# Token factors of two RMSNorms: from narrow sums, a 3-column root and row products to one wide product with a matrix of ones

## The chip, the cores and the metric

The kernel runs on one core of a Trainium2 chip. TensorE does the matrix products (weights are loaded into it beside the products), VectorE and ScalarE the operations on rows, GpSimd a few additions and some of the DMA issues, SyncE issues most DMAs. The metric is the device time of one execution in microseconds; lower is better. The times of before are three runs, 1497.79, 1493.73 and 1493.14 us, with the median 1493.73 us.

## The reference, cut to what matters

One step of a decoder trunk with one layer: a hybrid mixer, an attention into memory tokens, an MLP with squared ReLU, and a final norm. 1024 prompt tokens and 8 decode tokens go through the same weights, 1032 tokens in all. The model width is 1024, the hidden width 4096, and everything is f32. The change touches the two norms at the end:

```python
def rmsnorm(x, g):
    xf = x.astype(jnp.float32)
    y = xf * lax.rsqrt(jnp.mean(xf * xf, axis=-1, keepdims=True) + EPS)
    return (y * g.astype(jnp.float32)).astype(x.dtype)

def sq_relu_mlp(h, w_up, w_down):
    return jnp.square(jax.nn.relu(h @ w_up)) @ w_down

    ...
    xp = xp + sq_relu_mlp(rmsnorm(xp, norm_mlp[l]), w_up[l], w_down[l])
    ...
y_prompt = rmsnorm(xp, norm_final)
y_sample = rmsnorm(xd, norm_final)
```

Each token has one factor, 1 / sqrt(mean of its squares + EPS), which multiplies all 1024 of its values.

## The kernel before

**Layout.** Activations lie with the model width on the 128 partitions (8 tiles of 128) and the tokens along the columns. The 1032 tokens are four quarters of 258 columns (`QCOLS[0..3]`). A quarter pair is called a chunk `c`: chunk 0 has the quarters 0 and 1, chunk 1 the quarters 2 and 3. A token's factor must therefore come out as a row of numbers that stands on all 128 partitions.

**Products.** Every f32 operand is split into a high part and a low part (a rounding copy on ScalarE, written `UH`, `T_h` or the first half of `wu`, and a subtraction on VectorE, `UL`, `T_l`, the second half of `wu`), and each product is three passes: high by high, high by low, low by high. The MLP's two matrix products are done with a seven-product scheme over 2 x 2 blocks. `up_block(b, W, chunks)` runs the seven products of block b in the order 1, 6, 2, 7, 5, 4, 3. They share three PSUM banks: 1 and 2 add into X, 6, 7 and 4 into Z, 5 and 3 into Y. A product is 12 instructions of 258 columns (4 tiles of the width, 3 passes).

**What stands between the products (L2143).** After product 1, ScalarE copies X to `p` (L2194); product 2 adds into the same bank, so it must wait for that copy. After product 6, VectorE makes `u` from Z and `p` (L2197); product 7 adds into Z and must wait for `u`. Later results are added to `p` or `u` (L2206), multiplied by the factor row `ssum` under a ReLU (L2168), squared by ScalarE (`hq`), and combined into `ht` (L2176 to 2179), which goes to memory for the second matrix product.

**How the factor is made.** While the mixer's and the memory attention's result `pr_m` leaves PSUM, ScalarE squares each tile and GpSimd adds the squares, so that the quarter's 128 x 258 tile `ssum` holds one partial sum for each partition. `factor_columns` (L1979) multiplies that tile, as weights in three pieces of 86 tokens, by one column of ones (L1984): three narrow products that leave the token sums as a 86 x 3 block. ScalarE takes the root with the mean's scale and EPS as bias (L1988), VectorE the reciprocal (L1989), each on 3 columns. Later `factor_rows` turns that block into a row on all partitions with three products against an identity (through the helper, L75). `norm_rows` copies this row over `ssum` (L2004 in the function; on ScalarE). For the final norm VectorE multiplies from the PSUM bank directly.

**Where.** In the MLP, `norm_factor(0)` and `(1)` stand before the last of the `pr_m` products (n == 30), and their rows behind product 2 of block 0, chunk 0. Block 0 takes chunk 0 first, then come `norm_factor(2)` and `(3)`, the operands of chunk 1 (`first_half`, `second_half`), and block 0 for chunk 1 with its rows behind its product 2; from block 1 on both chunks run together. In the second matrix product (`dn`, L2309) the last of the output tiles `c` come at the program's end. `finish_columns` and `finish_rows` stand at four steps there (tables `COLUMNS_AT`, `ROWS_AT`, L2264), for each chunk and half of it: columns at steps 0, 3, 10 and 15, rows at 2, 5, 12 and 15. For the halves 1 the last tile's squares `sqt` are not added to `ssumf` but are multiplied by the ones in a second group of products into the same bank.

**What sets the order.** On TensorE the order is that of the text: `pin` keeps it so, and `pinned` and the helper `mm` hold the narrow and the row products in it. On ScalarE and VectorE a scheduler orders the instructions by its own estimate of when their operands are ready; so an edit can move instructions that it does not touch. Each engine then works off its own list in order and waits at its head.

Of the kernel before, what the change touches and what calls it, by code (L numbers as in the profile page):

```python
# [10 lines left out]
F32 = mybir.dt.float32  # L11
F32R = mybir.dt.float32r
I32 = mybir.dt.int32
AF = mybir.ActivationFunctionType
# [5 lines left out]
P = 128  # L20
D = 1024
# [5 lines left out]
QC = HALF // 2  # L27

QCOLS = [slice(h * HALF + c * QC, h * HALF + c * QC + QC) for c in range(2) for h in range(2)]
# [19 lines left out]
def decoder_step(ctx: ExitStack, tc: tile.TileContext, i: dict, o: dict):  # L49
    nc = tc.nc  # L50
# [10 lines left out]
    def pinned(ins):  # L61

        if pin[0]:
            tc.keep_in_program_order(ins)
# [9 lines left out]
    def mm(out, l, r, start, stop):  # L74
        pinned(nc.tensor.matmul(out, l, r, start=start, stop=stop))  # L75
# [20 lines left out]
    ones = G.tile([P, 1], F32, tag="ones", name="ones")  # L96
    nc.vector.memset(ones, 1.0)
    half = G.tile([P, 1], F32, tag="half", name="half")
# [182 lines left out]
    with pool("s") as A:  # L281
# [51 lines left out]
        ident = const("ident", [P, P])  # L333
# [12 lines left out]
        for t in range(9):  # L346
            n = P if t < 8 else 8
# [38 lines left out]
    with pool("a") as A:  # L386
# [29 lines left out]
        for t in range(9):  # L416
            q = A.tile([P, 512], F32, tag=f"qk{t}", name=f"qk_{t}")
# [1556 lines left out]
        nc.vector.tensor_sub(l, src, h.bitcast(F32))  # L1974


    QP = QC // 3

    def factor_columns(bank, sums, last, x):  # L1979
        col = bank[:QP, 300:303]  # L1980

        terms = [(y, j) for y in (sums, last) if y is not None for j in range(3)]
        for n, (y, j) in enumerate(terms):
            pinned(nc.tensor.matmul(  # L1984
                col[:, j : j + 1], y[:, j * QP : j * QP + QP], ones[:, :1], start=n == 0, stop=n >= len(terms) - 3,
                skip_group_check=True))
        fc = KC.tile([QP, 3], F32, tag=f"fc{x % 2}", name=f"fc_{x}", bufs=2)
        nc.scalar.activation(fc, col, AF.Sqrt, scale=1.0 / D, bias=epsc[:QP])  # L1988
        nc.vector.reciprocal(fc, fc)  # L1989
        return fc  # L1990

    def factor_rows(bank, fc):
        for j in range(3):
            mm(bank[:, j * QP : j * QP + QP], fc[:, j : j + 1].to_broadcast([QP, P]), ident[:QP, :QP], True, True)
        return bank[:, :QC]

    FACTORS = {}

    def norm_factor(x):
        fp = PD.tile([P, 512], F32, tag=("mk", "dt")[x % 2], name=f"rm_{x}", bufs=1)  # L2000
        FACTORS[x] = fp, factor_columns(fp, ssum[:, QCOLS[x]], None, x)

    def norm_rows(x):
        nc.scalar.copy(ssum[:, QCOLS[x]], factor_rows(*FACTORS[x]))  # L2004

    def first_half(c):

# [141 lines left out]
    def up_block(b, W, chunks):  # L2149
# [32 lines left out]
        for q in (1, 6, 2, 7, 5, 4, 3):  # L2182
            for c in chunks:
                if q in (1, 6, 5):
                    kind, d = {1: ("X", X), 6: ("Z", Z), 5: ("Y", Y)}[q]
                    d[c] = bank(kind, c)
                ps = (X if q in (1, 2) else Z if q in (6, 7, 4) else Y)[c]
                product(W, q, c, ps, q in (1, 6, 5))
                if b == 0 and q == 2:
                    norm_rows(2 * c)  # L2190
                    norm_rows(2 * c + 1)
                if q == 1:
                    p1[c] = small("p1", c)
                    nc.scalar.copy(p1[c], ps)  # L2194
                elif q == 6:
                    u2[c] = small("u2", c)
                    nc.vector.tensor_add(u2[c], ps, p1[c])  # L2197
                elif q == 2:
                    hidden(11, ps, c)
                elif q == 7:  # L2200
                    u3[c] = small("u3", c)
                    nc.vector.tensor_add(u3[c], ps, p1[c])
                else:
                    quad, x = {5: (22, u3), 4: (21, p1), 3: (12, u2)}[q]
                    r = small("r", f"{quad}_{c}", 4)
                    nc.vector.tensor_add(r, ps, x[c])  # L2206
                    hidden(quad, r, c)
# [33 lines left out]
    with pool("acc", side="right") as AC, pool("rd", side="right") as RD, pool("w") as A, pool("w_ps", space=PSUM) as PS:  # L2241
# [81 lines left out]
            nc.scalar.activation(sq, x, AF.Square)  # L2323
            (nc.vector if quad in (22, 12) else nc.gpsimd).tensor_add(ssf[:, cs], ssf[:, cs], sq)

        ends = {}

        def finish_columns(c, half):
            fp = PS.tile([P, 512], F32, tag=f"acc{turns[0] % 8}", name=f"fin_{c}_{half}", bufs=1)
            turns[0] += 1  # L2330
            ends[c, half] = fp, factor_columns(fp, ssf[:, QCOLS[2 * c + half]], tails[c] if half else None, 4 + 2 * c + half)
            for ft in range(8):
                y = C[((11, 21), (12, 22))[half][ft // 4]][:, ft % 4, c * QC : c * QC + QC]
                nc.scalar.activation(y, y, AF.Copy, scale=g_fin[:, ft : ft + 1])

        def finish_rows(c, half):
            cs = QCOLS[2 * c + half]
            rf = factor_rows(*ends[c, half])
            n = 2 if (c, half) == (1, 1) else 4
            for ft in range(0, 8, n):  # L2340
                y = C[((11, 21), (12, 22))[half][ft // 4]][:, ft % 4 : ft % 4 + n, c * QC : c * QC + QC]
                nc.vector.tensor_mul(y, y, rf.unsqueeze(1).to_broadcast([P, n, QC]))
                (nc.scalar if n == 2 and ft % 4 else nc.sync).dma_start(
                    o["yT"][ft * P : (ft + n) * P, cs].rearrange("(f p) c -> p f c", p=P), y)
# [282 lines left out]
```

## Time and profile before

| | |
|---|---|
| median of 3 runs | 1493.73 us (1493.14 to 1497.79) |
| span of the profiled execution | 1492.5 us |
| TensorE products | 1474.0 us busy, 99% of the span |
| TensorE weight loads (beside the products) | 1402.5 us, 94% |
| VectorE | 1102.5 us, 74% |
| ScalarE | 678.4 us, 45% |
| GpSimd | 325.4 us, 22% |

The profile gives the span of the profiled execution as its own time, from its first to its last instruction; the runs' times are taken on the device around the whole execution. Lines of the profile are read so: a start in us, a length in us, the engine, the line of the kernel, what is written `<-` what is read, the shape, and in brackets how long the engine stood idle before and what ended that. PE is TensorE, PEld its weight load, DVE VectorE, ACT ScalarE. In the chain of waits each row is a stretch on the chain that ended last: start, length, engine and what it did. In the groups by line, the two numbers behind the first bar are the group's busy us and the mean ns of one.

Of the places named above, `pr_m` ends and block 0 begins near 829 us, chunk 1 of block 0 runs from near 842 us, and the steps of the final norm stand between 1457 us and the end.

### The profile page before, as it was taken

Reading aid. Unit: us, or ns where it says so; the run is one execution under the profiler, and the core shown is the slowest. Engines: PE = TensorE matmul, PEld = TensorE weight load, DVE = VectorE, ACT = ScalarE, POOL = GpSimd, SP = SyncE. Lnnn points to the kernel's source line nnn. Section 1 sums busy time; section 2 is a strip of 40 time slices with the busy share of each in tenths; the row PEclk is TensorE's granted clock in tenths of the full one; section 3 lists DMA queues with packets and bytes.
Section 4 is the critical chain, followed back from the end, with each engine's and each line's share of the span. In section 5 each row is a group of like instructions: output and inputs, shape, how many; then the busy total and the mean of one; then the engine's idle time right before and its main releaser. Section 6 shows DMA issues by size and latency. Waiting matters only on the chain.

```text
span 1492.5 us, 27826 instructions
## 1 busy us (share of the span) xinstructions
PE 1474.0 (99%) x10893; PEld 1402.5 (94%) x10893; DVE 1102.5 (74%) x2279; ACT 678.4 (45%) x1326; POOL 325.4 (22%) x346
## 2 busy tenths in 40 slices
PE   9999999998999999999999999999999999999997
PEld 7899779998769999989999999999999999999997
DVE  7656636987877734567786978888888889787875
ACT  7534435665652432147535634334344444343454
POOL 0035323114414321104132000000001311020380
PEclk9999999999999999999999999999999999999999
DMA  8155737214857157483592443344436674536273
GB/s 292 61 186 168 201 71 181 80 34 123 232 181 279 49 191 193 132 238 103 165 321 72 128 149 137 141 156 157 142 141 210 237 265 142 172 99 191 81 129 114
DMA packets 125229, 236.67 MB, mean 159 GB/s; under 512 B 13744, under 2 KB 76517, under 8 KB 124970
## 3 DMA queue, kind: packets, MB, share of 16 engines
q1 hardware_dynamic: 89056, 170.50, 36.5%
q0 software_dynamic: 24912, 44.80, 10.9%
q10 hardware_dynamic: 11130, 19.60, 3.5%
q8 instruction: 85, 1.39, 0.4%
q14 instruction: 46, 0.38, 0.1%
HBM read 170.24 MB, written 57.52 MB: 153 GB/s over the span
## 4 chain that ended last, share of the span: by engine, by line
PE 90%; DVE 5%; ACT 2%; issue 1%; DMA 1%; ACTq 0%; POOL 0%; DVEq 0%; SPq 0%
PE dn L2309 21%; PE Z L2143 9%; PE qkp L75 7%; PE pr_o L75 6%; PE mq L75 6%; PE pr_m L75 6%; PE X L2143 6%; PE Y L2143 6%; PE grp L75 3%; PE sp L75 2%; PE av L75 2%; PE mv L75 2%; PE mk L75 1%; PE mpv L75 1%; PE vap_z L522 1%
## 5 line engine op out<-in xcount | busy, mean ns | idle before, releaser
L2309 PE MATMUL dn<-UH,wd 128*128 128x258 f32 x1792 | 324.6, 283 | 0.0
L2309 PEld LDWEIGHTS dn<-UH,wd 128*128 128x128 f32 x1792 | 277.5, 189 | 0.7 <-ACT c L2410 0.2
L2309 PE MATMUL dn<-UL,wd 128*128 128x258 f32 x896 | 252.8, 282 | 0.0
L2309 PEld LDWEIGHTS dn<-UL,wd 128*128 128x128 f32 x896 | 169.0, 189 | 0.0
L2413 DVE TENSOR_TENSOR c<-c,dn 128x258 f32<-128x258 f32 x216 | 88.9, 418 | 38.5 <-PE dn L2309 36.1
L2169 ACT ACTIVATE hq<-r 128x258 f32<-128x258 f32 x128 | 53.7, 421 | 118.3 <-DVE r L2168 118.3
L2143 PE MATMUL Z<-T_h,wu 128*128 128x258 f32 x512 | 98.2, 284 | 0.0
L2143 PE MATMUL X<-UH,wu 128*128 128x258 f32 x512 | 97.4, 282 | 0.0
L2287 ACT CAST wd<-raw_d 128x512 fp32r<-128x512 f32 x96 | 58.8, 620 | 79.0 <-PE dn L2309 74.6
L1953 ACT CAST wu<-raw_up 128x512 fp32r<-128x512 f32 x96 | 59.1, 617 | 59.9 <-PE Z L2143 50.0
L2280 ACT CAST UH<-raw_h 128x1032 fp32r<-128x1032 f32 x56 | 58.7, 1056 | 53.5 <-PE dn L2309 27.7
L2143 PEld LDWEIGHTS X<-UH,wu 128*128 128x128 f32 x512 | 81.3, 188 | 0.2 <-ACT p L2194 0.2
L2143 PEld LDWEIGHTS Z<-T_h,wu 128*128 128x128 f32 x512 | 81.3, 189 | 0.0
L2180 POOL DMA_DIRECT2D HT<-ht x32 | 17.2, 538 | 292.3 <-DVE ht L2179 291.8
L2281 DVE TENSOR_TENSOR UL<-raw_h,UH 128x1032 fp32r<-128x1032 f32 x56 | 73.6, 1315 | 8.6 <-ACT UH L2280 8.6
L2288 DVE TENSOR_TENSOR wd<-raw_d,wd 128x512 fp32r<-128x512 f32 x96 | 72.2, 759 | 10.0 <-ACT wd L2287 9.9
L2143 PE MATMUL Z<-T_l,wu 128*128 128x258 f32 x256 | 72.3, 282 | 0.0
L2143 PE MATMUL X<-UL,wu 128*128 128x258 f32 x256 | 72.3, 282 | 0.0
L128 ACT CAST wh_u<-raw_u 128x1024 fp32r<-128x1024 f32 x43 | 44.6, 1047 | 54.3 <-PE mq L75 31.1
L1954 DVE TENSOR_TENSOR wu<-raw_up,wu 128x512 fp32r<-128x512 f32 x96 | 64.7, 687 | 3.5 <-ACT wu L1953 3.5
L2301 POOL TENSOR_TENSOR raw_d<-raw_d,raw_d 128x512 f32<-128x512 f32 x16 | 22.1, 1383 | 193.8 <-DVE raw_d L2297 172.9
L129 DVE TENSOR_TENSOR wl_u<-raw_u,wh_u 128x1024 fp32r<-128x1024 f32 x39 | 49.4, 1273 | 18.8 <-ACT wh_u L128 18.6
(597 smaller groups left out, 4732.8 us busy)
## 6 DMA issues: line engine op xcount, KB each, us to landing
raw_u<-in_wall SPq DMA_DIRECT2D x49, 512.0 KB
HT<-ht POOLq DMA_DIRECT2D x32, 516.0 KB
raw_h<-HT SPq DMA_DIRECT2D x32, 516.0 KB
raw_up<-in_wall SPq DMA_DIRECT2D x32, 512.0 KB
raw_d<-in_wall SPq DMA_DIRECT2D x32, 512.0 KB
HQ<-hq ACTq DMA_DIRECT2D x32, 387.0 KB
raw_h<-HQ SPq DMA_DIRECT2D x24, 516.0 KB
cmk<-in_cmk SPq DMA_DIRECT2D x16, 512.0 KB
```

The lines of the kernel that those rows point to most:

```text
L75: pinned(nc.tensor.matmul(out, l, r, start=start, stop=stop))
L129: (lo_engine or nc.vector).tensor_sub(wl[:, :n], raw[:, :n], wh[:, :n].bitcast(F32))
L1953: nc.scalar.copy(w[:, :512], src)
L1954: nc.vector.tensor_sub(w[:, 512:], src, w[:, :512].bitcast(F32))
L2143: pinned(nc.tensor.matmul(ps, l, r[:, k, :], start=first and k == 0 and x == 0, stop=k == 3 and x == 2, skip_group_check=True))
L2169: nc.scalar.activation(h[:, PLACE[quad], :], r, AF.Square)
L2280: nc.scalar.copy(h, rv)
L2281: nc.vector.tensor_sub(l, rv, h.bitcast(F32))
L2287: nc.scalar.copy(w[:, :512], src)
L2288: nc.vector.tensor_sub(w[:, 512:], src, w[:, :512].bitcast(F32))
L2309: pinned(nc.tensor.matmul(ps, l, r[:, k, cq], start=first and k == 0 and x == 0, stop=k == 3 and x == 2, skip_group_check=True))
L2413: nc.vector.tensor_add(y, y, ps)
```

## The change

`factor_columns` and `factor_rows` give way to `token_factors`. One wide product with a 128 x 128 matrix of ones (`onesq`) as weights and the partial sums as its 258 columns leaves the token sums on all 128 partitions at once; for the halves 1 of the final norm a second such product adds the last tile's squares. ScalarE takes the root of the full 128 x 258 tile in place in PSUM, and VectorE writes the reciprocal of 128 x 258 from PSUM into the sums' own tile. So the rows are there without further products: the calls in `up_block` go away, and `finish_rows` multiplies from `ssf` in SBUF instead of a PSUM bank. The wide products stand where the narrow ones stood on TensorE. On TensorE, 24 narrow sums with 6 more for the tails become 8 wide ones with 2 more, all plain f32, and 24 row products go away. ScalarE's two copies a chunk into `ssum` go away as well.

```diff
--- before.py
+++ after.py
@@ -1974,34 +1974,17 @@
         nc.vector.tensor_sub(l, src, h.bitcast(F32))
 
 
-    QP = QC // 3
-
-    def factor_columns(bank, sums, last, x):
-        col = bank[:QP, 300:303]
-
-        terms = [(y, j) for y in (sums, last) if y is not None for j in range(3)]
-        for n, (y, j) in enumerate(terms):
-            pinned(nc.tensor.matmul(
-                col[:, j : j + 1], y[:, j * QP : j * QP + QP], ones[:, :1], start=n == 0, stop=n >= len(terms) - 3,
-                skip_group_check=True))
-        fc = KC.tile([QP, 3], F32, tag=f"fc{x % 2}", name=f"fc_{x}", bufs=2)
-        nc.scalar.activation(fc, col, AF.Sqrt, scale=1.0 / D, bias=epsc[:QP])
-        nc.vector.reciprocal(fc, fc)
-        return fc
-
-    def factor_rows(bank, fc):
-        for j in range(3):
-            mm(bank[:, j * QP : j * QP + QP], fc[:, j : j + 1].to_broadcast([QP, P]), ident[:QP, :QP], True, True)
-        return bank[:, :QC]
-
-    FACTORS = {}
+    def token_factors(bank, sums, last=None):
+        f = bank[:, :QC]
+        mm(f, onesq, sums, True, last is None)
+        if last is not None:
+            mm(f, onesq, last, False, True)
+        nc.scalar.activation(f, f, AF.Sqrt, scale=1.0 / D, bias=epsc)
+        nc.vector.reciprocal(sums, f)
 
     def norm_factor(x):
         fp = PD.tile([P, 512], F32, tag=("mk", "dt")[x % 2], name=f"rm_{x}", bufs=1)
-        FACTORS[x] = fp, factor_columns(fp, ssum[:, QCOLS[x]], None, x)
-
-    def norm_rows(x):
-        nc.scalar.copy(ssum[:, QCOLS[x]], factor_rows(*FACTORS[x]))
+        token_factors(fp, ssum[:, QCOLS[x]])
 
     def first_half(c):
 
@@ -2186,9 +2169,6 @@
                     d[c] = bank(kind, c)
                 ps = (X if q in (1, 2) else Z if q in (6, 7, 4) else Y)[c]
                 product(W, q, c, ps, q in (1, 6, 5))
-                if b == 0 and q == 2:
-                    norm_rows(2 * c)
-                    norm_rows(2 * c + 1)
                 if q == 1:
                     p1[c] = small("p1", c)
                     nc.scalar.copy(p1[c], ps)
@@ -2323,19 +2303,17 @@
             nc.scalar.activation(sq, x, AF.Square)
             (nc.vector if quad in (22, 12) else nc.gpsimd).tensor_add(ssf[:, cs], ssf[:, cs], sq)
 
-        ends = {}
-
         def finish_columns(c, half):
             fp = PS.tile([P, 512], F32, tag=f"acc{turns[0] % 8}", name=f"fin_{c}_{half}", bufs=1)
             turns[0] += 1
-            ends[c, half] = fp, factor_columns(fp, ssf[:, QCOLS[2 * c + half]], tails[c] if half else None, 4 + 2 * c + half)
+            token_factors(fp, ssf[:, QCOLS[2 * c + half]], tails[c] if half else None)
             for ft in range(8):
                 y = C[((11, 21), (12, 22))[half][ft // 4]][:, ft % 4, c * QC : c * QC + QC]
                 nc.scalar.activation(y, y, AF.Copy, scale=g_fin[:, ft : ft + 1])
 
         def finish_rows(c, half):
             cs = QCOLS[2 * c + half]
-            rf = factor_rows(*ends[c, half])
+            rf = ssf[:, cs]
             n = 2 if (c, half) == (1, 1) else 4
             for ft in range(0, 8, n):
                 y = C[((11, 21), (12, 22))[half][ft // 4]][:, ft % 4 : ft % 4 + n, c * QC : c * QC + QC]
```

ScalarE, around the copy `p` of block 0, chunk 0 (`fc` or `rm` is the root for the second quarter, `wu` a weight's high part, `xq_1` and `UH` the operands of chunk 1). Before:

```order
L1988 ACTIVATE fc_9033<-rm_9029,epsc 86x3
L1953 CAST wu_5_9090<-raw_up_1_9071 128x512
L1953 CAST wu_4_9093<-raw_up_1_9071 128x512
L2112 ACTIVATE xq_1_7880<-xs_3_9061,g_mlp 128x258
L2117 ACTIVATE sqc_m_3_9064<-xs_3_9061 128x258
L2119 DMA X_72<-xs_3_9061 128x258
L1953 CAST wu_3_9097<-raw_up_0_9070 128x512
L2194 COPY p_0_0_9148<-X_0_9135 128x258
L1973 CAST UH<-xq_1_7880 128x2x258 x2
```

Now:

```order
L1982 ACTIVATE rm_9026<-rm_9026,epsc 128x258
L1953 CAST wu_5_9084<-raw_up_1_9065 128x512
L1953 CAST wu_4_9087<-raw_up_1_9065 128x512
L1953 CAST wu_3_9091<-raw_up_0_9064 128x512
L1973 CAST UH<-xq_1_7880 128x2x258
L1953 CAST wu_1_9405<-raw_up_0_9400 128x512
L2095 ACTIVATE xq_1_7880<-xs_3_9055,g_mlp 128x258
L2100 ACTIVATE sqc_m_3_9058<-xs_3_9055 128x258
L2102 DMA X_72<-xs_3_9055 128x258
L1973 CAST UH<-xq_1_7880 128x2x258
L2174 COPY p_0_0_9142<-X_0_9129 128x258
```

Three rows more stand between the root and the copy: the cast `wu_1`, which was behind it, and two halves of `UH`.

VectorE, from chunk 0's last add in block 0 (`r_12`) to chunk 1's `u`. Before:

```order
L2206 TENSOR_TENSOR r_12_0_9248<-Y_0_9203,u_0_0_9163 128x258
L1989 RECIPROCAL fc_9263<-fc_9263 86x3
L1989 RECIPROCAL fc_9270<-fc_9270 86x3
L2168 SCALAR_TENSOR_TENSOR r_12_0_9248<-r_12_0_9248,ssum_7881 128x258
L1974 TENSOR_TENSOR T_l<-t_1_9281,T_h 128x516
L2021 TENSOR_TENSOR xq_1_7878<-xq_1_7878,t_1_9280 128x516
L1974 TENSOR_TENSOR UL<-xq_1_7880,UH 128x2x258
L2197 TENSOR_TENSOR u_0_1_9332<-Z_1_9319,p_0_1_9317 128x258
L1974 TENSOR_TENSOR T_l<-xq_1_7878,T_h 128x516
L1954 TENSOR_TENSOR wu_1_9433<-raw_up_0_9428,wu_1_9433 128x512
L2176 TENSOR_TENSOR ht_0_9253<-hq_0_9185 128x258
```

Now:

```order
L2186 TENSOR_TENSOR r_12_0_9234<-Y_0_9189,u_0_0_9157 128x258
L2004 TENSOR_TENSOR xq_1_7878<-xq_1_7878,t_1_9260 128x516
L2151 SCALAR_TENSOR_TENSOR r_12_0_9234<-r_12_0_9234,ssum_7881 128x258
L1983 RECIPROCAL ssum_7881<-rm_9245 128x258
L1983 RECIPROCAL ssum_7881<-rm_9249 128x258
L1974 TENSOR_TENSOR T_l<-t_1_9261,T_h 128x516
L1974 TENSOR_TENSOR T_l<-xq_1_7878,T_h 128x516
L1974 TENSOR_TENSOR UL<-xq_1_7880,UH 128x2x258
L2159 TENSOR_TENSOR ht_0_9239<-hq_0_9171 128x258
L2161 TENSOR_TENSOR ht_0_9239<-hq_0_9171 128x258
L2160 TENSOR_TENSOR ht_0_9239<-hq_0_9171,ht_0_9239 128x258
L2177 TENSOR_TENSOR u_0_1_9312<-Z_1_9299,p_0_1_9297 128x258
```

The two reciprocals are of 258 columns and stand behind the factor's multiplication, and `u` of chunk 1 is behind three `ht` rows and the second `T_l`, which it was ahead of.

VectorE at the end, from the last adds of `c` to the first multiplication of the last half. Before:

```order
L2413 TENSOR_TENSOR c_13390<-c_13390,dn_5_1_1_17185 128x258
L2413 TENSOR_TENSOR c_13390<-c_13390,dn_5_2_1_17202 128x258
L2324 TENSOR_TENSOR ssumf<-ssumf,sqc_f_1_1_17290 128x258
L2324 TENSOR_TENSOR ssumf<-ssumf,sqc_f_2_1_17306 128x258
L2413 TENSOR_TENSOR c_13390<-c_13390,dn_5_3_1_17237 128x258
L1989 RECIPROCAL fc_17331<-fc_17331 86x3
L2342 TENSOR_TENSOR c_13390<-c_13390,fin_1_17324 128x2x258 x2
```

Now:

```order
L2391 TENSOR_TENSOR c_13362<-c_13362,dn_5_1_1_17145 128x258
L2391 TENSOR_TENSOR c_13362<-c_13362,dn_5_2_1_17162 128x258
L2304 TENSOR_TENSOR ssumf<-ssumf,sqc_f_1_1_17242 128x258
L2391 TENSOR_TENSOR c_13362<-c_13362,dn_5_3_1_17192 128x258
L2304 TENSOR_TENSOR ssumf<-ssumf,sqc_f_2_1_17258 128x258
L1983 RECIPROCAL ssumf<-fin_1_17276 128x258
L2320 TENSOR_TENSOR c_13362<-c_13362,ssumf 128x2x258 x2
```

The add of the squares `sqc_f_2` stands behind the last add of `c` (`dn_5_3`), ahead of which it was.

## The prediction

> **What bounds the kernel now.** I read the page first: which engine is busy, and the chain of work that ended last.
>
> ```profile
> span 1492.5 us, 27826 instructions
> PE 1474.0 (99%) x10893; PEld 1402.5 (94%) x10893; DVE 1102.5 (74%) x2279; ACT 678.4 (45%) x1326; POOL 325.4 (22%) x346
> ...
> PE 90%; DVE 5%; ACT 2%; issue 1%; DMA 1%; ACTq 0%; POOL 0%; DVEq 0%; SPq 0%
> ```
>
> TensorE bounds the program, so a product taken off its list is worth its time, unless another engine then becomes late. The span is 1492.5 us against a median of 1493.73, so 1.2 us lie outside it; I forecast a difference and put it on the median. The second view is the chain in order of time, cut to the two places that the diff touches (start, length, what).
>
> ```profile
> 833.85 1.30 PE rm L75 x12
> 835.16 1.48 PE Z L2143 x12
> 836.64 1.44 PE Y L2143 x12
> ...
> 841.00 0.85 PE rm L1984 x12
> 841.85 1.54 PE X L2143 x12
> ...
> 846.26 1.30 PE rm L75 x12
> ```
>
> ```profile
> 1457.21 0.39 PE fin L1984 x6
> 1457.60 2.99 PE dn L2309 x24
> 1460.59 0.63 PE fin L75 x6
> 1461.22 1.48 PE dn L2309 x12
> ...
> 1483.29 0.43 ACT sqt L2317
> ...
> 1483.76 0.63 PE fin L1984 x6
> ...
> 1484.42 0.27 ACT fc L1988
> ...
> 1484.71 0.18 DVE fc L1989
> ...
> 1484.94 0.91 PE fin L75 x6
> ...
> 1485.87 0.69 DVE c L2342
> ```
>
> Everything that the change replaces on TensorE lies on this chain. Only at the very end, behind TensorE's last product, do others take it over, and there every step of the factor is on it.
>
> **Removed from TensorE: the products that write the factors out as rows.** A pair costs 1.30 us, and the product behind it 1.48 instead of 1.44: 1.34. A single one costs 0.63 + 0.04 = 0.67. Two pairs in the MLP and three single ones before the tail: 2 x 1.34 + 3 x 0.67 = 4.7 us. The fourth, at the end, belongs to the tail below.
>
> **Exchanged on TensorE: narrow sums for wide ones.** The narrow ones of a pair (x12, since an f32 product is two passes) cost 0.85 and another 0.10 in the product behind (1.54 for 1.44), 0.95 in all; those of a single place (x6) cost 0.39 + 0.11 (2.99 for two of 1.44), 0.50. A wide sum is a plain f32 product of 128 rows and 258 columns. The trace has none of that width, but it has one of 512 in the middle of a steady stream:
>
> ```profile
> 456.03 1.02 PE L75 MATMUL rp<-diag,onesb 128*128 128x512 f32 x2
> 456.49 0.72 PE L75 MATMUL pr_o<-UH,wh_u 128*128 128x344 f32 x1
> 457.04 0.32 PE L75 MATMUL pr_o<-UL,wh_u 128*128 128x344 f32 x1
> 457.20 0.32 PE L75 MATMUL pr_o<-UH,wl_u 128*128 128x344 f32 x1
> ```
>
> The stream's pitch is 0.16 us (457.04 to 457.20). From 456.03 to 457.04 stand the f32 product and one member of the stream: 1.01 less 0.16. So 512 columns cost 0.85 us in two passes, and 258 cost 0.43. Bounds: 0.43 by columns, up to 0.85 if the length did not count. I take 0.43, since in these passes the time is all columns. Two sums or an accumulated pair are then 0.86 for 0.95, a single one 0.43 for 0.50: 0.4 us less over all places. TensorE's list is 5.1 us shorter. That is the most that the change can bring ahead of the tail; the rest is who becomes late.
>
> **Added: a root and a reciprocal of 258 columns instead of 3.** ScalarE has an operation like the new root, in place in PSUM with a bias column; VectorE has short reciprocals and plain operations of both widths:
>
> ```profile
> L1801 ACT ACTIVATE ms<-ms,mmn 128x256 f32<-128x256 f32 x32 | 14.4, 450 | 3.7 <-DVE mmn L1797 3.2
> L1988 ACT ACTIVATE fc<-rm,epsc 86x3 f32<-86x3 f32 x4 | 1.0, 255 | 0.9 <-PE rm L1984 0.9
> ```
>
> ```profile
> L2413 DVE TENSOR_TENSOR c<-c,dn 128x258 f32<-128x258 f32 x216 | 88.9, 418 | 38.5 <-PE dn L2309 36.1
> L1014 DVE RECIPROCAL mn<-sm 128x1 f32<-128x1 f32 x32 | 5.1, 159 | 2.4 <-ACT e L1007 1.7 <-issue 0.5
> L1068 DVE RECIPROCAL c<-sm 128x8 f32<-128x8 f32 x4 | 0.8, 188 | 0.0
> L2021 DVE TENSOR_TENSOR xq<-xq,t 128x516 f32<-128x516 f32 x2 | 1.4, 684 | 0.0
> ```
>
> The root: 0.45 us for 0.26. The reciprocal decides this case and has no row near its width. A plain operation costs (684 - 418) / 258 = 1.0 ns a column and 0.42 us at 258. The reciprocal goes from 159 to 188 ns over 7 columns, 4.1 ns a column, so 0.155 + 258 x 0.0041 = 1.22 us. Lower bound 0.42 (a plain operation). [...] A dozen ns in the short rows may be jitter, which leaves 0.9 to 1.7 as my own range. I take 1.22.
>
> [...]
>
> **The MLP's first block, first chunk.** TensorE's own order has product 2 add into X's bank behind product 6, so product 2 waits for ScalarE's copy `p` of X.
>
> ```profile
> 829.33 0.24 ACT L1988 ACTIVATE fc<-rm,epsc 86x3 f32<-86x3 f32 x1
> 829.47 0.61 ACT L1953 CAST wu<-raw_up 128x512 fp32r<-128x512 f32 x1
> 829.98 0.62 ACT L1953 CAST wu<-raw_up 128x512 fp32r<-128x512 f32 x1
> ...
> 831.74 0.37 ACT L2194 COPY p<-X 128x258 f32<-128x258 f32 x1
> ...
> 832.15 0.19 PEld L2143 LDWEIGHTS X<-UH,wu 128*128 128x128 f32 x1 [0.23 <-ACT p L2194]
> ```
>
> It already waits 0.23 us. ScalarE has no gap between 829.33 and the copy. The new order, shown ahead, puts three more casts in front of the copy (two halves of `xq`, and the next block's first weight), each 0.52 us after the other by the two casts above, and the second root is 0.2 longer (the first one's extra falls into a wait). The copy starts at 831.74 + 1.56 + 0.2 = 833.5, and product 2 at 833.95 instead of 832.15: 1.8 us late. The removed pair gives 1.34 back: the chunk is **0.45 us late**, with 0 gained. Queued behind the copy are the casts for chunk 1, needed six products later; the reciprocals themselves stand on VectorE ahead of nothing that this product needs, as long as they are under about 1.7 us each.
>
> **Second chunk.** Product 7 adds into Z's bank and needs VectorE's `u`, which reads Z, and the low part `T_l`.
>
> ```profile
> 841.28 0.42 DVE L2206 TENSOR_TENSOR r<-Y,u 128x258 f32<-128x258 f32 x1
> ...
> 842.58 0.68 DVE L1974 TENSOR_TENSOR T_l<-t,T_h 128x516 fp32r<-128x516 f32 x1
> 843.19 0.69 DVE L2021 TENSOR_TENSOR xq<-xq,t 128x516 f32<-128x516 f32 x1
> ...
> 844.93 0.43 DVE L2197 TENSOR_TENSOR u<-Z,p 128x258 f32<-128x258 f32 x1 [0.45 <-PE Z L2143]
> ...
> 846.82 0.42 DVE L2178 TENSOR_TENSOR ht<-hq 128x258 f32<-128x258 f32 x1
> ...
> 847.35 0.37 PE L2143 MATMUL Z<-T_h,wu 128*128 128x258 f32 x1
> ```
>
> Operations of 516 columns follow each other at 0.61 us (842.58 to 843.19), 0.07 to 0.08 less than their length; those of 258 so at 0.34. The new order has, from chunk 0's last add (its product ends 0.4 later, so 841.45): the add 0.34, `xq` 0.61, the factor 0.34, two reciprocals of 1.22 - 0.08 = 1.14, three operations of 0.61, three `ht` of 0.34, then `u`. That starts `u` at 847.9 and ends it at 848.3; product 7 starts there instead of 847.35. **The MLP is 0.9 us longer**, although 2.9 us (2 x 1.34 + 2 x 0.09) came off TensorE. Behind this, weights for the next block have 3 us to spare, so nothing more is lost.
>
> **The end.** TensorE's last product ends 2.0 us earlier (three row products; sums equal). VectorE gets two more long reciprocals ahead of it, which its waits between 1457 and 1478 take up. From the last add of `c` the tail changes so: the last sum now stands behind that add and not before it, so that the first wide product ends 0.3 after the square is ready; the root is 0.2 longer, the reciprocal 1.05, and the row product with its hand-over (1484.94 to 1485.87) is gone, 0.95. Together 0.6 longer: **the end gains 2.0 - 0.6 = 1.4 us.** The multiplications and the last DMA behind them are the same.
>
> Sum: +0.9 - 1.4 = -0.5 us: 1493.73 - 0.5 = **1493.2 us**, no change.
>
> **Rivals.**
>
> *A, the waits hide: everything taken off TensorE arrives.* This needs the copy `p` and chunk 1's `u` to be on time after all. For it: TensorE waits only 0.23 us there now. Against it: both are placed behind long work in a queue. Time: -2.9 - 1.4 = -4.3 us, 1489.4; with a plain-priced reciprocal 0.8 less.
>
> [...]
>
> *C, the reciprocal is a plain operation, 0.42 us.* The first chunk stays late by ScalarE (+0.45), the second gains 0.6 on that (-0.2 in all), the end gains 2.1: -2.3 us, 1491.4. Against it: 188 ns, where a plain operation of 8 columns would have 418 - 250 x 1.03 = 160.
>
> **Chances.** My forecast with reciprocals from 0.9 to 1.7 us (-1.4 to +1.6): 0.65. A 0.08, B 0.13, C 0.14. A measurement here can tell 0.3%, 4.5 us, from no change. A is at that bound, so nearly all of its share counts as faster; B is beyond it. Faster 0.07, same 0.80, slower 0.13. Range: the forecast's own -1.4 to +1.6, C at -2.3, and some way towards A and B, with 1 us for the runs: 1490.3 to 1498.0.
>
> **What would show it.** No row products; the eight `rm` and `fin` sums at 0.43 us pitch; RECIPROCAL 128x258 near 1.2 us (0.4: C; over 2: B); the copy `p` near 833.5 and TensorE's wait for it near 2 us; a second wait near 1.9 us for VectorE's `u` ahead of chunk 1's product 7; the first weight load of the second block 0.9 us later than now; 0.6 us more from the last add to the first multiplication. The forecast is wrong if these waits are not there (A) or if VectorE keeps TensorE waiting in later blocks as well.

## The result

The change made the kernel a little slower, by some 0.4%. In the first comparison its median was 1501.45 us (six runs, 1495.35 to 1505.66) against 1494.41 us before (six runs), a ratio of 1.0038 (95% interval 1.0024 to 1.0051). Repeated on one chip it was 1502.36 us against 1495.14, a ratio of 1.0042 (1.0030 to 1.0055). The prediction was 1493.2 us and no change, with a range of 1490.3 to 1498.0. The time lies outside it. (The ratio given is not the quotient of the two medians, which is 1.0047.)

The profiled execution of the changed kernel ran 1495.35 us, with a span of 1493.6. That is 6 us under its own median, so this one profile shows only a part of the loss. The page, its first lines:

```profile
span 1493.6 us, 27645 instructions
PE 1469.9 (98%) x10805; PEld 1397.8 (94%) x10805; DVE 1111.0 (74%) x2279; ACT 679.2 (45%) x1322; POOL 323.4 (22%) x346
```

TensorE has 4.1 us less to do (1474.0 before), as it should, and the span is 1.1 us longer. The groups of VectorE by shape give the price that the prediction lacked (count, then busy us and mean ns of one):

```profile
L1983 DVE RECIPROCAL ssumf<-fin 128x258 f32<-128x258 f32 x4 | 7.1, 1768 | 2.2 <-ACT fin L1982 2.2
L1983 DVE RECIPROCAL ssum<-rm 128x258 f32<-128x258 f32 x4 | 6.8, 1731 | 0.0
L1068 DVE RECIPROCAL c<-sm 128x8 f32<-128x8 f32 x4 | 0.8, 190 | 0.0
```

The wide reciprocal takes 1.73 to 1.77 us, not 1.22. From 1 to 8 columns it costs (190 - 159) / 7 = 4.4 ns a column, from 8 to 258 it costs (1731 - 190) / 250 = 6.2.

The timeline of TensorE in block 0, the rows before which it stood idle (the bracket is the wait and what ended it):

```profile
832.61 0.39 PE L2126 MATMUL X<-UH,wu 128*128 128x258 f32 x1 [1.81 <-ACT p L2174]
835.27 0.39 PE L2126 MATMUL Z<-T_h,wu 128*128 128x258 f32 x1 [0.94 <-DVE u L2177]
849.22 0.39 PE L2126 MATMUL Z<-T_h,wu 128*128 128x258 f32 x1 [2.69 <-DVE u L2177]
```

Three waits, 5.4 us in all. Before, the same stretch had one of 0.23 us. What stood ahead of the first one, from the timelines of ScalarE and of VectorE:

```profile
829.91 0.62 ACT L1973 CAST UH<-xq 128x516 fp32r<-128x516 f32 x1
830.43 0.62 ACT L1953 CAST wu<-raw_up 128x512 fp32r<-128x512 f32 x1
...
830.96 0.51 ACT L2095 ACTIVATE xq<-xs,g_mlp 128x258 f32<-128x258 f32 x1
...
831.68 0.61 ACT L1973 CAST UH<-xq 128x516 fp32r<-128x516 f32 x1
832.19 0.37 ACT L2174 COPY p<-X 128x258 f32<-128x258 f32 x1
```

```profile
827.16 3.38 DVE L1983 RECIPROCAL ssum<-rm 128x258 f32<-128x258 f32 x2
830.46 0.36 DVE L2092 TENSOR_TENSOR xs<-pr_m,xq 128x258 f32<-128x258 f32 x1
...
842.67 3.39 DVE L1983 RECIPROCAL ssum<-rm 128x258 f32<-128x258 f32 x2
...
848.74 0.42 DVE L2177 TENSOR_TENSOR u<-Z,p 128x258 f32<-128x258 f32 x1
```

Two pairs of reciprocals hold VectorE for 3.4 us each, in a stretch where it had no gap to take them up. Counted on TensorE from block 0's first product to block 1's, block 0 takes 27.29 us instead of 24.09: **3.2 us more**. The first product of each block, before (L2143) and after (L2126):

```profile
829.10 0.28 PE L2143 MATMUL X<-UH,wu 128*128 128x258 f32 x1
...
853.19 0.28 PE L2143 MATMUL X<-UH,wu 128*128 128x258 f32 x1
```

```profile
827.78 0.28 PE L2126 MATMUL X<-UH,wu 128*128 128x258 f32 x1
...
855.07 0.28 PE L2126 MATMUL X<-UH,wu 128*128 128x258 f32 x1
```

The chain of waits at the end:

```profile
1459.48 0.44 PE fin L75 x2
...
1482.87 0.04 DVE c L2391
...
1483.21 0.43 DVE ssumf L2304
...
1483.69 1.15 PE fin L75 x4
...
1484.86 0.46 ACT fin L1982
...
1485.35 1.78 DVE ssumf L1983
...
1487.15 0.70 DVE c L2320
```

From the last add of `c` to the first multiplication it is 1487.15 - 1482.87 = 4.28 us. Before, the last add started here:

```profile
1482.84 0.42 DVE L2413 TENSOR_TENSOR c<-c,dn 128x258 f32<-128x258 f32 x1
```

So there it was 1485.87 - 1482.84 = 3.03. The tail is 1.25 us longer. From block 1's first product to that last add it is 627.80 us instead of 629.65, 1.85 us less: that is what the row products gave. The end is 0.6 us shorter in all, and block 0 and the end together make the kernel 2.6 us slower. (The span grew by only 1.1, because block 0 began 1.3 us earlier in this execution, of which the exchanged sums explain 0.1.)

So 2.6 us can be read in the profile, and the median lost 7. The rest is not in a list of instructions, and the first experiment was made to find it.

### The profile page after: what moved, and what is told of

Read it like the earlier page. It is cut to its first block, busy times and chain, and to the rows that moved or that the text cites. A ratio compares the mean times of both kernels' runs of the same rounds, so it can differ in the third digit from the quotient of the medians.

```text
span 1493.6 us, 27645 instructions
## 1 busy us (share of the span) xinstructions
PE 1469.9 (98%) x10805; PEld 1397.8 (94%) x10805; DVE 1111.0 (74%) x2279; ACT 679.2 (45%) x1322; POOL 323.4 (22%) x346
## 4 chain that ended last, share of the span: by engine, by line
PE 88%; DVE 8%; ACT 2%; issue 2%; DMA 0%; ACTq 0%; POOL 0%; another core or an unknown queue 0%; DVEq 0%
PE dn L2289 21%; PE Z L2126 8%; PE qkp L75 7%; PE pr_o L75 6%; PE mq L75 6%; PE Y L2126 5%; PE X L2126 5%; PE pr_m L75 4%; PE grp L75 3%; PE sp L75 2%; PE av L75 2%; PE mv L75 1%; PE mk L75 1%; PE mpv L75 1%; PE vap_z L522 1%
## 5 line engine op out<-in xcount | busy, mean ns | idle before, releaser
L2391 DVE TENSOR_TENSOR c<-c,dn 128x258 f32<-128x258 f32 x216 | 88.2, 416 | 35.0 <-PE dn L2289 32.6
L2126 PE MATMUL Z<-T_h,wu 128*128 128x258 f32 x512 | 98.3, 284 | 3.6 <-DVE u L2177 3.6
L2126 PE MATMUL X<-UH,wu 128*128 128x258 f32 x512 | 97.5, 282 | 1.8 <-ACT p L2174 1.8
L2126 PEld LDWEIGHTS Z<-T_h,wu 128*128 128x128 f32 x512 | 81.3, 189 | 4.0 <-DVE u L2177 4.0
L2126 PEld LDWEIGHTS X<-UH,wu 128*128 128x128 f32 x512 | 81.3, 188 | 2.0 <-ACT p L2174 2.0
L2126 PE MATMUL Z<-T_l,wu 128*128 128x258 f32 x256 | 72.3, 282 | 0.0
L2126 PE MATMUL X<-UL,wu 128*128 128x258 f32 x256 | 72.3, 282 | 0.0
L75 PE MATMUL qkp<-UH,wh_u 128*128 128x344 f32 x192 | 63.1, 329 | 0.1
```

Source lines behind the costliest of these rows:

```text
L2126: pinned(nc.tensor.matmul(ps, l, r[:, k, :], start=first and k == 0 and x == 0, stop=k == 3 and x == 2, skip_group_check=True))
L2391: nc.vector.tensor_add(y, y, ps)
```

## The experiments

Each time is a median of runs that alternate with the kernel before. "Clock" is the mean granted TensorE clock of a run. In 65 such runs of the kernel before it was never below 0.995.

### The change once more, with its clocks

> The changed kernel as it is, once more beside the kernel before. The profile of the change showed RECIPROCAL 128x258 at 1.73 to 1.77 us, the MLP's first block 3.2 us longer (from the last pr_m product to block 1's first product), the end 0.6 us shorter, together +2.6 us; but the median of six runs was 7 us above before, and the runs over 1500 us had a granted clock of 0.991 to 0.996 where the others had 0.997. Theory H: TensorE's wait of 2.7 us for VectorE's u in block 0, chunk 1 is long enough that the throttle lowers the clock behind it in some runs: the runs of the change stand in two groups, near before +2.6 and near before +8 to +10 with a clock near 0.991, and runs of before don't. Rival N: the dips of the clock belong to waits elsewhere, in code that the change leaves alone: before shows them as often, and the difference is +2.6 us.

Measured: 1502.36 us (12 runs, 1495.12 to 1504.42) against 1495.14. Eight of the 12 runs had a clock of 0.991 to 0.994, and all eight are at 1500.85 us or more; three of the other four, at 0.996 or 0.997, are at 1495.1 to 1497.3. Its profile is of a run at 0.991 (1503.45 us), which shows where the clock goes. Its busy time by stretch, and in the last columns the granted clock, the DMA share and GB/s (the pairs are TensorE, its weight loads, VectorE, ScalarE and GpSimd, each busy us with its number of instructions):

```profile
836.20:843.10 6.90, 6.16 (x30) 5.86 (x29) 5.10 (x10) 2.71 (x5) 0.00 (x0) 0.51 0.32 125
843.10:853.30 10.20, 8.10 (x64) 7.78 (x63) 9.97 (x17) 3.90 (x9) 0.00 (x0) 1.00 0.35 110
853.30:860.10 6.80, 6.21 (x29) 6.21 (x30) 4.68 (x11) 1.04 (x2) 0.60 (x1) 0.50 0.68 207
```

```profile
834.90 0.39 PE L2126 MATMUL X<-UH,wu 128*128 128x258 f32 x1 [1.81 <-ACT p L2174]
...
853.89 0.58 PE L2126 MATMUL Z<-T_h,wu 128*128 128x258 f32 x1 [2.69 <-DVE u L2177]
```

These two waits are as long as in the first profile. But here the clock falls to half (0.51 and 0.50) for 6.9 and 6.8 us, once 1.3 us behind the wait of 1.81 and once in the wait of 2.69. In the first of the two 30 products are done where the first profile, in the same window, has 56. Block 0 takes 830.07 to 862.47, 32.40 us: 5.1 more than in the first profile. The first profile had the waits and not the falls:

```profile
836.20:843.10 6.90, 6.90 (x56) 6.79 (x55) 6.90 (x15) 3.68 (x8) 0.00 (x0) 1.00 0.05 21
843.10:853.30 10.20, 7.51 (x63) 7.30 (x62) 10.20 (x18) 2.93 (x7) 0.60 (x1) 1.00 0.72 201
```

2.6 us from the lists and 5.1 from the clock where it falls twice are 7.7; the median lost 7.2. This speaks for theory H, that the waits bring the clock down, but does not yet separate the waits from what else is new there. H had named only the wait of 2.7 us; the one of 1.81 us has a fall behind it as well.

Rival N is answered by the clocks, since none of the 29 runs of before in this comparison is at 0.994 or less. But not every fall belongs to the change. Of the ten profiles whose clock was read in steps of 10 us over the span, eight have one step at 0.83 between 350 and 370 us, in the attention, which is 3.4 us at half; the kernel before and the one with only quarters 2 and 3 wide have none. In the first profile it begins at 353.4 us, in a wait of TensorE of 2.29 us, in the repeat at 354.9, behind one of some 2.2. Six of all eleven have half clock near 788 us. The change touches neither place, and the profiles of the end alone and of the copy below have such falls too. The one at 788.4 us in this profile has no long wait ahead of it, only one of 0.26 us among products of 8 columns:

```profile
785.90 0.75 PE L75 MATMUL pr_m<-UH,wh_u 128*128 128x258 f32 x4 [0.26 <-ACT UH L2053]
786.49 1.40 PE L75 MATMUL opm<-selgt,daccm 128*128 128x8 f32 x12
```

This profile's block 0 begins 2.3 us later than the first one's (830.07 and 827.78); 3.4 us at half clock account for some 1.7 of that, an estimate from half the work in that time.

### One half of the change at a time

```diff
 # the MLP's norm alone: norm_factor as changed, the rows behind product 2 gone, finish_* as before
-        FACTORS[x] = fp, factor_columns(fp, ssum[:, QCOLS[x]], None, x)
+        token_factors(fp, ssum[:, QCOLS[x]])
 # the final norm alone: finish_columns and finish_rows as changed, norm_factor as before
-            rf = factor_rows(*ends[c, half])
+            rf = ssf[:, cs]
```

> Wide sums, root and reciprocal in front of the MLP alone; the final norm as before. By both theories the first block is 3.2 us longer and nothing is given back at the end: +3.2 us in the profile. H: the low clocks (near 0.991) are here as in the full change, and the median is +6 or more. N: no more low clocks than before, median +3.2.

> Wide sums, root and reciprocal in the final norm alone; the MLP as before. By both theories -2.2 us up to TensorE's last product and +1.6 from the last add of c to the first multiplication: -0.6 us. H: clocks as before (0.997 and up), since no long wait of TensorE is added. N: clocks like those of the full change.

Measured: the MLP alone 1502.88 us, a ratio of 1.0054 (1.0039 to 1.0070), with half of its six runs at a clock of 0.992 or 0.993; its profile has half clock behind the same two waits (1.89 and 2.67 us), for 6.8 and 3.4 us, and block 0 takes 31.10 us. The end alone 1495.15 us, a ratio of 1.0003 (0.9994 to 1.0012), all clocks 0.995 or more. So the whole loss is in the MLP's part. The interval of the end alone holds the 0.6 us that were forecast for it, and no gain at all as well.

### The reciprocal's length taken away

```diff
-        nc.vector.reciprocal(sums, f)
+        nc.vector.tensor_copy(sums, f)
```

> The full change with VectorE's reciprocal replaced by a copy of the same 128x258 from PSUM (leaves out the reciprocal, so the factors are their inverses). If the reciprocal's 1.75 us is what the prediction had wrong, this is its rival C: first block from +3.2 to about 0, end -2.2 + 0.3, in all -2.0 to -2.5 us against before; TensorE's wait ahead of product 7 in chunk 1 falls from 2.69 to below 1 us. H: no clock below 0.997. If the first block stays over +2, the reordered lists and not the reciprocal's length make it late.

This kernel leaves out the reciprocal, so its factors are the inverses of the right ones; it shows a time and nothing else. Measured: 1491.36 us, a ratio of 0.9984 (0.9973 to 0.9995), all 12 clocks 0.995 or more. The waits of TensorE in block 0:

```profile
833.64 0.39 PE L2126 MATMUL X<-UH,wu 128*128 128x258 f32 x1 [0.22 <-ACT p L2174]
845.22 0.38 PE L2126 MATMUL X<-UH,wu 128*128 128x258 f32 x1 [0.32 <-ACT p L2174]
```

The copy takes 0.42 us in place of 1.73. Block 0 falls to 22.25 us, 1.8 less than before, since now most of what came off TensorE arrives. The two copies `p` are nearly on time, and no wait for `u` is left. This was the prediction's rival C, -2.3 us; measured is -3.8 between the medians and -2.4 by the ratio. One limit of this run: with the short operation the scheduler also put ScalarE's casts back behind `p`, so it takes away the long reciprocals and the new order of ScalarE's list together. On VectorE too the order is another: chunk 1's `u` stands ahead of the three `ht` operations that were ahead of it in the change. In the profile of the change either the long reciprocals or ScalarE's order is enough to make `p` late (ScalarE has no gap ahead of 832.19, and `xs`, which it needs, comes at 830.82 from behind the reciprocals). No run separates these.

### Which pair of reciprocals

```diff
+        if x < 2:                     # quarters 0 and 1: columns and rows as before
+            FACTORS[x] = fp, factor_columns(fp, ssum[:, QCOLS[x]], None, x)
+        else:                         # quarters 2 and 3: wide
+            token_factors(fp, ssum[:, QCOLS[x]])
```

> Before, with the wide form only for the quarters 2 and 3 of the MLP's norm (the two reciprocals that stand ahead of chunk 1's u); quarters 0 and 1 and the final norm as before. My theory: no wait for p over 0.3 us and none for u in chunk 0; the wait ahead of product 7 in chunk 1 stays at 2 to 2.7 us, so one half-clock stretch instead of two in some runs: +1.5 us where the clock holds, +4 to +5 where it does not, median +2 to +4. If the two waits came from the first two reciprocals (VectorE simply carried its lateness on from chunk 0), chunk 1's wait is below 1 us and the time is that of before.

Measured: 1497.33 us, a ratio of 1.0012 (1.0001 to 1.0022). In the profile one wait of TensorE is left:

```profile
846.95 0.39 PE L2154 MATMUL Z<-T_h,wu 128*128 128x258 f32 x1 [1.31 <-DVE u L2208]
```

It lies between the two expectations, but it does not split the 2.69 us between the two pairs. VectorE comes to the second pair 1.5 us earlier than in the change, counted from block 0's first product (842.03 - 828.61 against 842.67 - 827.78), and its list is another one as well: `u` starts 1.15 us after the two reciprocals (846.48, from 845.33), where in the change a second `T_l` and three `ht` more stood between, and it was 2.76 us (848.74, from 845.98). This profile has block 0 at 24.22 us, 0.1 over before, and full clock there. The runs stand in two groups, five at 1494.5 to 1495.6 (clock 0.997 and up) and six at 1497.3 to 1499.3 (0.995 or 0.996). Whether the upper group is again a fall of the clock is open: its clocks are ones that before has at 1495 us too, and no trace of it was taken.

### Is it the waiting? The waits filled

```diff
+                if b == 0:
+                    for _ in range({(2, 0): 12, (7, 0): 6, (7, 1): 18}.get((q, c), 0)):
+                        pinned(nc.tensor.matmul(
+                            seen["fp"][:, 258:512], W[1][:, 0:P], RIGHT[1, c][0][:, 0, 0:254], start=True, stop=True,
+                            skip_group_check=True))
                 product(W, q, c, ps, q in (1, 6, 5))
```

> The full change, with 36 products that nobody reads on TensorE's list in block 0, in the places where it stood idle: 12 ahead of product 2 and 6 ahead of product 7 in chunk 0, 18 ahead of product 7 in chunk 1 (0.12 us each, 1.4, 0.7 and 2.2 us, a little less than the waits of 1.81, 0.94 and 2.69). No wait for the other engines gets shorter by it. H (the clock falls to half because TensorE did nothing for some 2 us): no half clock between 830 and 862 us, all runs near before +2.6, median some 1497.5 instead of 1502. Rival W (the clock falls for another reason, the products of plain f32 or the work of VectorE): half clock as before the filling, median 1502 or more.

> The full change, with the 18 products that nobody reads ahead of product 7 in chunk 1 alone (2.2 us in a wait of 2.69), where ScalarE's and VectorE's lists up to u stay those of the change. The wait of 1.81 us in chunk 0 stays. H: the half clock near 853 us goes, that near 836 us stays in a part of the runs; some 3 us less than the change in the runs of low clock, median 1498 to 1500, and no clock below 0.993. W: clocks of 0.991 to 0.993 in half of the runs or more, as in the change, and a median of 1502.

The second keeps only the 18 products ahead of chunk 1's product 7. Both failed as tests by the time: 1507.8 us (ratio 1.0095, 1.0080 to 1.0111) and 1506.78 us (1.0072, 1.0058 to 1.0086), slower than the change. The scheduler, seeing more work on TensorE, put other operations of VectorE ahead, so the waits moved instead of going away. The traces still tell something, since the fall of the clock moved with them. With all three filled, TensorE's waits and the stretches:

```profile
835.10 0.39 PE L2127 MATMUL X<-UH,wu 128*128 128x258 f32 x1 [0.34 <-ACT p L2180]
837.76 0.39 PE L2127 MATMUL Z<-T_h,wu 128*128 128x258 f32 x1 [0.25 <-DVE u L2183]
847.76 0.58 PE L2127 MATMUL Z<-T_h,wu 128*128 128x258 f32 x1 [6.85 <-DVE u L2188]
```

```profile
833.00:843.40 10.40, 7.32 (x56) 6.64 (x55) 10.40 (x19) 5.33 (x12) 1.20 (x1) 1.00 0.32 114
843.40:853.70 10.30, 5.94 (x26) 5.85 (x27) 6.32 (x13) 1.68 (x4) 0.00 (x0) 0.50 0.40 132
```

Behind the filled places (0.34 and 0.25 us left) the clock stays whole; behind the new wait of 6.85 us it is half for 10.3 us. With only chunk 1's wait filled:

```profile
836.30 0.39 PE L2127 MATMUL X<-UH,wu 128*128 128x258 f32 x1 [1.89 <-ACT p L2180]
...
855.42 0.39 PE L2127 MATMUL Z<-T_h,wu 128*128 128x258 f32 x1 [0.57 <-DVE u L2183]
861.59 0.52 PE L2127 MATMUL Z<-T_h,wu 128*128 128x258 f32 x1 [3.03 <-DVE u L2188]
```

```profile
837.80:844.70 6.90, 5.96 (x28) 5.70 (x27) 5.06 (x11) 2.56 (x5) 0.00 (x0) 0.51 0.33 119
844.70:861.70 17.00, 13.40 (x107) 12.87 (x106) 16.65 (x30) 6.50 (x14) 0.60 (x1) 1.00 0.46 148
861.70:865.10 3.40, 3.40 (x16) 3.40 (x17) 2.35 (x6) 1.01 (x2) 0.00 (x0) 0.50 0.17 27
```

Half clock behind 1.89, none behind 0.57, half again behind the new wait of 3.03, although the wide products and reciprocals are all still there. Filling a wait on one engine's list is no clean experiment where a scheduler orders the others.

### Is it the waiting? One wait added to the kernel before

```diff
+                if (b, q, c) == (0, 2, 0):
+                    idle = KC.tile([P, 8], F32, tag="idle8", name="idle8")
+                    nc.gpsimd.tensor_tensor(idle, p1[c][:, 0:8], p1[c][:, 0:8], op=ALU.mult)
+                    nc.gpsimd.tensor_tensor(idle, idle, minus_half[:, 0:1].to_broadcast([P, 8]), op=ALU.pow)
+                    pinned(nc.tensor.matmul(
+                        FACTORS[0][0][:8, 400:401], idle, ones[:, :1], start=True, stop=True, skip_group_check=True))
                 product(W, q, c, ps, q in (1, 6, 5))
```

> Before, with one wait of TensorE added and nothing else: two operations of 8 columns on GpSimd, which is idle there, start from p of block 0, chunk 0 (a product of p with itself, then a power, which took 2.55 us at 8 columns), and a product of one column that nobody reads waits for them on TensorE's list ahead of product 2. ScalarE's and VectorE's lists are those of before. No wide product, no long reciprocal. H: TensorE is idle some 2.5 to 3 us there; in a part of the runs a stretch of half clock of 3.4 or 6.8 us follows, so the runs stand in two groups, near before +3 with a clock of 0.996 and near before +5 to +6.5 with 0.994 or less; median +3 to +6. W (the clock falls by the wide products or by VectorE's work): all runs near +3, no clock below 0.995.

This one leaves the lists of ScalarE and VectorE untouched. Measured: 1498.58 us, a ratio of 1.0021 (1.0012 to 1.0030). Seven runs have clocks of 0.996 to 0.998 and lie at 1495.3 to 1499.1; four have 0.994 or 0.995 and lie at 1499.8 to 1500.9. The profile is of the second kind:

```profile
835.21 0.20 PE L2193 MATMUL rm<-ones,idle 128*8 128x1 f32 x2 [2.64 <-POOL idle L2192]
```

```profile
835.10:838.50 3.40, 3.29 (x17) 3.27 (x18) 0.67 (x2) 0.11 (x1) 0.05 (x1) 0.50 0.34 134
```

Block 0 takes 28.23 us, 4.1 over before. The wait accounts for 2.64 - 0.23 = 2.4 of it and 3.4 us at half clock for 1.7. With no wide product and no long reciprocal in the kernel, the clock falls to half at 835.10, in the wait that was added, and is whole again from 838.50. So in this execution a wait of TensorE of 2.64 us was enough to bring the clock down: W is not needed, and H is shown as far as that. Three limits stand. The loss of time, 2.97 us between the medians, is at the lower edge of what H forecast; only one of the four runs of low clock has a profile; and a wait is not the only way to a fall, since this profile too has one near 787.3 us (0.86 from 780 to 790), where the repeat has it behind the products of 8 columns.

### The wide form at three of the end's four places

```diff
+            if (c, half) == (1, 1):
+                ends[c, half] = fp, factor_columns(fp, ssf[:, QCOLS[2 * c + half]], tails[c], 4 + 2 * c + half)
+            else:
+                token_factors(fp, ssf[:, QCOLS[2 * c + half]], tails[c] if half else None)
...
+            rf = factor_rows(*ends[c, half]) if (c, half) == (1, 1) else ssf[:, cs]
```

> Before, with the wide form in the final norm for three of its four places, (0,0), (1,0) and (0,1), whose root and reciprocal lie beside TensorE's last products; the last place (1,1), where every step of the factor is on the chain, keeps the narrow sums and rows, and the MLP is as before. TensorE's last product ends 2.0 to 2.2 us earlier, the tail from the last add to the first multiplication stays at 2.6 us (+0.3 where the last sum stands behind the last add): -1.8 us against before, a ratio of 0.9988. Rival: the long reciprocals make VectorE late for the last adds, and the tail gives it back (0.9996 or more).

Measured: 1493.01 us against 1495.23, a ratio of 0.9987 (0.9976 to 0.9998), where 0.9988 was expected; the interval ends just short of 1. The end of its chain:

```profile
1480.37 0.04 DVE c L2424
...
1481.18 1.09 PE fin L1984 x12
...
1483.76 0.69 DVE c L2353
```

From the last add to the first multiplication it is 3.39 us, against 4.28 in the change and 3.03 before. Of the places that were tried, the wide form gained only here, where TensorE is the bound and VectorE has room: in the profile of before they are busy 21.0 and 13.8 of the 21 us from 1457 to 1478.

## Why the prediction was wrong

**Removed and exchanged on TensorE: right.** A wide sum costs 0.44 us (0.43 forecast), no row product is left, and from block 1 to the last add the end gained 1.85 us where 2.0 were forecast. In block 0, without its waits, TensorE has 24.09 - 0.23 = 23.9 us of work before and 27.29 - 5.44 = 21.9 after, 2.0 us less where 2.8 were forecast. The missing 0.8 belong to the waits. The product ahead of the first wait starts at 830.52 and the second one behind it at 832.83, 2.31 us for two steps of 0.12, so this wait costs 2.07 us and not 1.81; the other two also cost 0.26 and 0.27 more than their length.

**The reciprocal's price: the first step that failed, a term that was mis-sized.** The prediction took 1.22 us from a slope between 1 and 8 columns, with 0.9 to 1.7 as its own range; it is 1.73 to 1.77. It had written that the first chunk's reciprocals hold up nothing "as long as they are under about 1.7 us each", so the truth fell just on the other side of its own border. What failed is "a dozen ns in the short rows may be jitter, which leaves 0.9 to 1.7": a slope over 7 columns was carried over 250. From 8 to 258 columns the runs show 6.2 ns a column, against (683 - 416) / 258 = 1.0 for a plain operation (L2004 and L2391 of the change).

**First chunk: right in place, half right in size.** Against block 0's first product, `p` starts 4.41 us later after and 2.64 before, so 1.77 us late where 1.8 was forecast, and TensorE waits 1.81. A wait that the forecast did not have came as well: the one of 0.94 us for `u`.

**Second chunk: right in place, short in size.** TensorE waits for `u` as forecast, 2.69 us and not 1.93; the two reciprocals alone are 1.0 us longer than assumed. So the MLP is 2.8 us of work less and 6.0 us of waits more, +3.2, where the prediction had 2.8 less and some 3.7 more, +0.9.

A view of the kernel before that the prediction did not read would have bounded this without any order. By stretches of block 0, the third pair of numbers is VectorE's busy time:

```profile
826.00:836.00 10.00, 9.97 (x85) 9.77 (x85) 8.57 (x16) 9.19 (x22) 1.93 (x3) 1.00 0.42 141
836.00:843.00 7.00, 7.00 (x65) 7.00 (x64) 6.49 (x16) 2.96 (x9) 0.00 (x0) 1.00 0.02 8
843.00:850.00 7.00, 7.00 (x62) 7.00 (x61) 6.33 (x14) 2.99 (x7) 0.60 (x1) 1.00 0.79 230
```

In these 24 us VectorE is busy 21.4 and has 2.6 to give; four reciprocals bring 4 x (1.73 - 0.16) = 6.3.

**The end.** +1.25 us on the tail instead of +0.6; 0.55 of the difference is the reciprocal. So the end gained 0.6 us, not 1.4. By the lists alone the sum would have been +2.6 us instead of -0.5: 1496.3 us, inside the range and within 0.3%.

**The second step that failed: the clock, a term put at nothing.** The prediction costed a wait of TensorE at its own length, at the granted clock of 0.998 that the profile of before has. In the profiles of the change and its halves a wait of some 2 us can cost its length and then a stretch of half clock: in the repeat 6.9 and 6.8 us of it come with the waits of 1.81 and 2.69 us, in the MLP alone 6.8 and 3.4 us with those of 1.89 and 2.67; with the added wait of 2.64 us it was 3.4. Eight of the repeat's 12 runs have a clock of 0.991 to 0.994. In the repeat's profile this is 5.1 of the 7.7 us, the greater part, and the one that took the time out of the range. The last sentence on what would prove the forecast wrong named waits in later blocks; nothing in it named the clock. The traces show when the clock falls and not why: in steps of 0.1 us, the falls in the repeat's profile start at 788.4, 836.2 and 853.3 us, 14 and 5 times 3.41 apart. How long a wait may be was not shown either: those of 1.81 and 1.89 us were followed by half clock, those of 1.81 and 2.69 in the first profile were not.

**Rivals.** A fell by the waits. C's time was nearly met by the copy in place of the reciprocal, 2.4 us gained by the ratio (3.8 between the medians) against a predicted 2.3, but not all of its mechanism: it kept the first chunk late by ScalarE, and with the copy the scheduler put the casts back and that lateness went. B, a reciprocal of over 2 us, has a share in the chances and in the range, but no run shows that price: the runs showed 1.73 to 1.77 us, and VectorE was late in both chunks (TensorE waited 0.94 and 2.69 us for `u`). The 0.13 that B got was too little. The forecast's own +1.6 us at 1.7 us a reciprocal was the author's estimate and is in no run; by the lists it was +2.6 at 1.73 to 1.77.

## What to carry to other kernels

The reciprocal on VectorE was paid by the column here: 168 ns at 86x3, between 163 at 128x2 and 171 at 128x4, and 1731 at 128x258. To spread a sum over 128 partitions first and invert it then turns 3 columns into 258; ask whether VectorE has 1.7 us to give before each of them is needed. Where TensorE is the bound, cost a new wait of it not only by its length: waits of 1.81 to 2.69 us were followed by 3.4 to 6.9 us of half clock here in some executions, so add that, and read several profiles, since one may have missed it. Before moving work to an engine with a low share over the whole span, look at its gaps in the stage concerned: VectorE was at 74% over the program and had 2.6 of 24 us free where four reciprocals wanted 6.3.

## What the runs showed of the hardware that was not expected

- Half clock came in stretches of 3.4, 6.8 to 6.9 and 10.3 us, near one, two and three times 3.41. Within one execution the starts lay whole multiples of 3.413 us apart: 354.91, 788.40, 836.19 and 853.26 us in the repeat (127, 14 and 5 times), 360.28, 790.36, 838.14 and 855.21 in the MLP alone (126, 14 and 5 times), 353.43 and 1486.65 in the first profile (332 times). The hundredths are estimates, from the mean clock of the step of 0.1 us in which each fall lies. Counted back from 836.19 by 3.413, the repeat's wait of 1.81 us (833.09 to 834.90) lies inside one such stretch, 832.78 to 836.19, and half clock followed; counted on from 353.43 by 140 times 3.4133, a stretch of the first profile ends at 831.29, within the same wait (830.80 to 832.61), and none followed. Whether this is what makes the spread of one program from 1495 to 1504 us was not tried.
- In the repeat a fall came without a long wait: near 788 us the clock fell to half behind 16 instructions of 8 columns (785.13 to 787.74), with a wait of 0.26 us among them; six of the eleven profiles have a fall near there. That the few columns are the reason was not tried.
- What sets apart a wait with half clock behind it from one without was not settled. In the repeat the 1.81 us that lay inside one stretch of 3.413 were followed by half clock. In the first profile 1.83 of the 2.69 us (846.53 to 848.36), counted on from 353.43 us, lay in one stretch, and the clock stayed whole, 1.00 from 843.1 to 860.1; but the ends of products in a trace are modelled, so the two numbers may not differ.
- The reciprocal's price per column rises: 4.4 ns from 1 to 8 columns and 6.2 from 8 to 258, reading PSUM in the wide case and SBUF at 1 and 8. One narrow row reads PSUM (L845, 128x4) and takes 170 ns, in line with 162 at 2 columns and 190 at 8 from SBUF, which speaks for the width and not the source; a wide one from SBUF was not tried.
